# Output projection of a hybrid encoder layer on one Trainium2 core: a PSUM bank of its own for the second half of each normalized tile's transposition, both halves one product later, and three gating steps later

## Chip, core and metric

The kernel runs on one core of one Trainium2 chip. The metric is device time in microseconds (us). The engines are named as in the profile: PE is the matrix engine (PEld its weight loads), DVE the vector engine, ACT the scalar engine, POOL the GpSimd engine, SP the engine that issues most DMAs. PSUM, where PE writes its results, has eight banks of 128 x 512 numbers here.

## What is computed

The reference is one encoder layer over 1280 tokens (256 and 1024) of width 1024:

```python
h = rmsnorm(x, attn_norm_g)
proj = h @ w_in
a = mla_group(...)            # latent attention, 8 heads
b = na_group(...)             # neighbourhood attention, 8 heads
mix = concatenate([rmsnorm(a, mla_out_g), rmsnorm(b, na_out_g)])
x = x + mix @ w_o             # output projection
h2 = rmsnorm(x, ffn_norm_g)
x = x + (silu(h2 @ w_gate) * (h2 @ w_up)) @ w_down
y = rmsnorm(x, final_norm_g)
```

The change lies between `mix @ w_o` and the first products with `w_gate` and `w_up`.

## The kernel before

Every matmul operand is kept as a high and a low part, and one product is three matmuls (`mm3`, lines 111 to 113). Tokens go in ten tiles of 128. The instructions of ACT, DVE and POOL are put in order by a scheduler when the kernel is built; PE's order is as written from the second turn of the output projection to the end of the first feed-forward run. Each engine executes its own queue strictly in order; engines wait for one another by semaphores. The names below are those of the profile.

**Output projection.** Turn t (t from 0 to 9) of a loop multiplies tile t's mixed, transposed activations `mT` with `wo`: 16 products `at` = 0 to 15, each of three matmuls into bank `po` (two buffers; the first eight products fill one half of the columns, the last eight the other). A dictionary `between` says what PE does after which product. In turn t that is, for the next tile's mixed activations, the transposition of a first half after product 1 and of a second half after product 5 (four 128 x 128 transposes each, line 898, into the single bank `trm`), which ACT (line 900) and DVE (line 901) read out; and for the tile before, t - 1, the transposition of its normalized activations `h2`, again in two halves, after products 9 and 12 (line 957, into the single bank `trh`). DVE multiplies the first half into the feed-forward input `x` (line 961), ACT the second half (line 967).

What the normalized tile needs is a chain over four engines: PE ends the tile's products, DVE adds the residual (line 930), ACT squares and sums (line 941), POOL makes the factor `rh` (lines 90 and 92), DVE scales the tile (line 944), and only then PE can transpose. POOL's queue holds much other work in this stage, above all weight operands for the feed-forward (lines 1064, 1069, 1071). DVE's queue holds sums over tiles (lines 984 and 992) as well. For the last two tiles the second half goes into `trm`; the last tile's two halves come when the feed-forward run has begun, in `xm_in`.

**Feed-forward.** Gate and up products come in runs of 20 pairs (steps `at`), a run for each of the two matrices and each block of columns; they use a seven-fold scheme with sums of operands (`S`, made by `build_S`), and PSUM banks `M` (pools `pm0` and `pm1`, four buffers each; `pm1` takes the banks that `po`, `trm` and `trh` had). DVE adds what a bank holds into the result tile `C` (line 1239), ACT copies where the result is first written (line 1241). `C` has three buffers. While the run after the first two goes on (n = 0 in `plan`), DVE works through the gating of the finished pair: `act_step` (lines 1266 and 1272) with the numbers in `STEPS_1`, each ordered after the eviction next to it, and SP stores the results (`act_d`). One bank of `M`, called `junk`, is held during the output projection as a dump for ACT's squares (line 881).

Of the kernel before, what the change touches and what calls it, by code (L numbers as in the profile page):

```python
# [12 lines left out]
F32 = mybir.dt.float32  # L13
# [6 lines left out]
P = 128  # L20
# [3 lines left out]
NT = NTOK // P  # L24
# [16 lines left out]
def encoder_trunk(ctx: ExitStack, tc: tile.TileContext, x_tm, x_T, g_attn, w_c, w_v, w_qk,  # L41
# [14 lines left out]
    def pool(name, bufs=1, side=None, space=None):  # L56
        kw = {"reuse_waits": "tile"}
        if side:
            kw["side"] = side
        if space:  # L60
            kw["space"] = space
        return tc.alloc_tile_pool(name=name, bufs=bufs, **kw)

    def load(out, in_):
        nc.sync.dma_start(out=out, in_=in_)

    def store(out, in_):
        nc.scalar.dma_start(out=out, in_=in_)
# [7 lines left out]
    def load_r(out, in_):  # L76
        nc.sync.dma_start(out=out.bitcast(F32), in_=in_.bitcast(F32))
# [10 lines left out]
    def rstd_of(out, ss, n):  # L88
        w = out.shape[1]
        nc.gpsimd.tensor_scalar(out=out, in0=ss, scalar1=1.0 / n, scalar2=EPS,  # L90
                                op0=ALU.mult, op1=ALU.add)
        return nc.gpsimd.tensor_tensor(out=out, in0=out, in1=mhalf[:, 0:w], op=ALU.pow).ins
# [70 lines left out]
    def load_x(t):  # L163
        x = rx.tile([P, D], F32, name="x", bufs=2)
        load(x, x_tm[t * P:(t + 1) * P, :])
        return x
# [684 lines left out]
    po = pool("po", space=PSUM, side="right")  # L851
# [6 lines left out]
    def load_wo(n, pl, nm):  # L858
        raws = pl.tile([P, 2, D], F32, name=nm)
        for j in range(2):  # L860
            kc, raw = 2 * n + j, raws[:, j]
            load(raw, w_o[kc])
            nc.gpsimd.tensor_scalar(out=raw, in0=raw, scalar1=gm[:, kc:kc + 1], scalar2=1.0,
                                    op0=ALU.mult, op1=ALU.mult)
            wt = rw.tile([P, 2, D], F32R, name=f"wo{kc}")
            split_w(wt[:, 0], wt[:, 1], raw)
            wo.append(wt)
# [23 lines left out]
    def mix_T(t, mn):  # L891
        mT = (rt1 if t % 2 else rt0).tile([P, 2, KC, P], F32R, name=f"mT{t % 2}")

        def half(q):
            tr = po.tile([P, 4, P], F32, name="trm", bufs=1)
            for i in range(4):
                kc = 4 * q + i
                nc.tensor.transpose(tr[:, i], mn[:, kc * P:(kc + 1) * P], ident)
            hi, lo = mT[:, 0, 4 * q:4 * q + 4], mT[:, 1, 4 * q:4 * q + 4]
            last_split[0] = nc.scalar.copy(out=hi, in_=tr).ins  # L900
            last_low[0] = nc.vector.tensor_sub(out=lo, in0=tr, in1=hi).ins

        return mT, half
# [33 lines left out]
    def ffn_in(t, x):  # L937
        h2 = rm.tile([P, D], F32, name="m", bufs=3)
        ss = rm.tile([P, 1], F32, name="ssh", bufs=2)
        r = rm.tile([P, 1], F32, name="rh", bufs=2)  # L940
        nc.scalar.activation(h2, x, AF.Square, accum_out=ss)
        store(xm_d[t], x)
        normed[0] = rstd_of(r, ss, D)
        scaled[0] = nc.vector.tensor_scalar(out=h2, in0=x, scalar1=r, scalar2=1.0, op0=ALU.mult,
                                            op1=ALU.mult).ins
        cuts, a = [], t * P
        while a < (t + 1) * P:
            j = a // XC
            e = min((j + 1) * XC, (t + 1) * P)
            cuts.append((j, slice(a - j * XC, e - j * XC), slice(a - t * P, e - t * P)))  # L950
            a = e

        def half(q):
            tr = po.tile([P, 4, P], F32, name="trm" if t >= NT - 2 and q else "trh", bufs=1)
            for i in range(4):
                kc = 4 * q + i
                tp = nc.tensor.transpose(tr[:, i], h2[:, kc * P:(kc + 1) * P], ident)
            for j, to, of in cuts:
                if q == 0:
                    for k in range(2):  # L960
                        ev[0] = nc.vector.tensor_mul(
                            out=X[k, j][:, :, to], in0=tr[:, 2 * k:2 * k + 2, of],
                            in1=gf[:, 2 * k:2 * k + 2].unsqueeze(2).to_broadcast(
                                [P, 2, of.stop - of.start])).ins
                else:
                    for i in range(4):
                        nc.scalar.activation(X[2 + i // 2, j][:, i % 2, to], tr[:, i, of],
                                             AF.Copy, scale=gf[:, 4 + i:5 + i])
            return tp.ins

        return half
# [61 lines left out]
    pm = [pool("pm0", space=PSUM)]  # L1033
    for n, (pl, nm) in enumerate(((rw, "wo4"), (rw, "wo5"), (rw, "wo6"), (rt0, "mT0"))):
        load_wo(n, pl, nm)
    junk = [None, pm[0].tile([P, 512], F32, name="M0", bufs=4)]
    cur, half = mix_T(0, mix_in(0))
    half(0)
    half(1)
# [46 lines left out]
    last_half = None  # L1086
    for t in range(NT):
        if t == 1:
            pe_order.enter_context(tc.manual_schedule(engines={mybir.EngineType.SP,
                                                               mybir.EngineType.PE}))  # L1090
        if t + 2 < NT:
            with tc.issue_after(last_split[0]):
                coming = mix_in(t + 2)
        x = load_x(0) if t == 0 else x_next
        x_next = load_x(t + 1) if t + 1 < NT else None
        for job in kept:
            load_r(*job)
        kept.clear()
        if t < 3:
            k = (slice(4, 6), slice(0, 4), slice(6, 8))[t]  # L1100
            for i in range(2):
                load(raw[:, i, k], src[i][0][:, k])
        with tc.issue_after(mixed[0]):
            for _ in range(2 if 1 < t < 6 else 1):
                next(early, None)
        jobs = JOBS.get(t, (None,) * 3)
        halves_[0] = t < NT - 1
        if t == NT - 1:
            with tc.issue_after(scaled[0]):
                for job in SECOND[4:5] + SECOND[6:]:  # L1110
                    job()
        between = {}
        if t + 1 < NT:
            nxt, half_m = mix_T(t + 1, ahead)

            def second_m(half_m=half_m, jobs=jobs):
                half_m(1)
                behind_now(last_low[0], jobs[0])

            between[1] = lambda: half_m(0)  # L1120
            between[5] = second_m
        if t:
            def first_h(half=last_half, jobs=jobs):
                half(0)
                behind_now(ev[0], jobs[2])
                if t == 8:
                    behind_now(ev[0], jobs[3])

            between[9 if t < 9 else 8] = first_h
            between[12 if t < 9 else 11] = lambda half=last_half: half(1)  # L1130
        if t < NT - 1:
            between[7] = lambda jobs=jobs: behind_now(added[0], jobs[1])
        out_proj(t, cur, x, between)
        if t == NT - 1:
            break
        last_half = ffn_in(t, x)
        with tc.issue_after(normed[0]):
            next(early, None)
            if t == 8:
                third_2(gps, slice(0, 168))  # L1140
        cur, ahead = nxt, coming
# [12 lines left out]
    last_half = ffn_in(9, x)  # L1154

    def xm_in(q):
        last_half(q)
        if q == 0:
            return
        for p_ in reversed(r3):  # L1160
            p_.release()
        po.release()
        pm.append(pool("pm1", space=PSUM, side="right"))
        l4.append(pool("l4t"))
# [163 lines left out]
    for at in range(20):  # L1328
        if at and at + 3 < 20:
            load_r(ring[(at + 3) % 4], wop_d[SEQ0[at + 3][0]])  # L1330
        if at in (5, 7):
            load_raw(1, at == 7)
        if at in BUILD:
            with tc.issue_after(evicted[0]):
                build_S(BUILD[at])
        w = ring[at % 4]
        for i, C in enumerate((G, U)):
            product(C, chains[i], written[i], SEQ0, at, (w[:, 0, i], w[:, 1, i]), BANK.get(at))
            if (at, i) in ((2, 1), (3, 0)):
                xm_in(at - 2)  # L1340
    pe_order.close()
    gate(G, 1)
    gate(G, 0)
# [91 lines left out]
    def advance(now):  # L1435
        while done[0] < len(jobs):
# [8 lines left out]
            if k == 8 and m + 2 < len(plan):  # L1445
# [3 lines left out]
    STEPS = {(0, 0): ((0, 1), 3), (0, 1): (1,), (0, 2): (7,), (0, 4): (2,), (0, 8): (5,),  # L1449
             (0, 12): (6,), (1, 12): ("22", 4), (1, 16): ("12",), (1, 18): ((0, 0),),  # L1450
             (1, 19): ((0, 2),)}
    STEPS_1 = {1: ("22", 4), 2: ("12",), 4: (7,), 8: ("11", 3), 10: (1,), 12: ("21",), 16: (2,)}
    STEPS_2 = {1: (5,), 4: (6,)}
    for n, (fp, i) in enumerate(plan):
        C = new_C()
# [12 lines left out]
        for at in range(20):  # L1468
# [7 lines left out]
            product(C, chains, written, seq, at, w)  # L1476
            steps_ = () if last_one else STEPS_1.get(at, ()) if n == 0 else STEPS.get((i, at), ())
            with tc.issue_after(evicted[0]):
# [302 lines left out]
```

## Time and profile before

| | us |
|---|---|
| three timed runs | 1599.02, 1597.18, 1597.21; median 1597.21 |
| profiled execution, its own time | 1599.25 |
| its span, first to last instruction | 1597.2 |

| engine | busy us of the span | share |
|---|---|---|
| PE | 1559.9 | 98% |
| DVE | 1015.4 | 64% |
| ACT | 761.1 | 48% |
| POOL | 766.1 | 48% |

The output projection lies at about 660 to 803 us of the span, the first feed-forward run at 803 to 850, the run n = 0 at 850 to 875. Timeline rows of the profile give start and duration in us, engine, line, operation, output from inputs, shapes and count, and in brackets the idle time ahead of the row with what ended it.

### The profile page before, as it was taken

The page shows a single profiled execution, that of the slowest core. Times are in us where ns is not written, and L with a number is a line of the kernel's source. Part 1 is how long each engine was busy: PE and PEld are TensorE (multiplying, and loading weights), DVE is VectorE, ACT ScalarE, POOL GpSimd, SP SyncE. Part 2 cuts the span into 40 slices and gives each one's busy share as a digit, 9 for nine tenths or more (in the row PEclk, how much of TensorE's full clock was granted, in tenths as well). Part 3 has the DMA queues.
Part 4 walks back from the last instruction along what each step waited for, and adds up shares of the span by engine and source line. Part 5 has one row for each costly group of instructions (what it writes and reads, how often), then busy time and mean ns, then how long its engine had stood idle before and what let it go on. Part 6 is the DMA issues. An engine that isn't in the chain of part 4 may idle for free.

```text
span 1597.2 us, 23983 instructions
## 1 busy us (share of the span) xinstructions
PE 1559.9 (98%) x8560; PEld 1395.4 (87%) x8560; DVE 1015.4 (64%) x1656; ACT 761.1 (48%) x1552; POOL 766.1 (48%) x961
## 2 busy tenths in 40 slices
PE   8999999999999999998999999999999999999998
PEld 8888789998888888877798999999999988888886
DVE  5754034566777777535588666566766665886676
ACT  6533144555677777633344444444344453443334
POOL 4633235544211119369536887788888871010002
PEclk9999999999999999999999999999999999999999
DMA  8626022253101030276473222223322237843434
GB/s 292 200 73 167 17 55 62 38 175 100 32 16 31 21 101 29 87 256 216 157 256 112 93 94 86 80 107 111 103 85 94 86 131 278 293 125 100 150 104 156
DMA packets 118022, 190.38 MB, mean 119 GB/s; under 512 B 34960, under 2 KB 65424, under 8 KB 115344
## 3 DMA queue, kind: packets, MB, share of 16 engines
q1 hardware_dynamic: 85216, 162.64, 31.2%
q10 hardware_dynamic: 31872, 23.14, 4.6%
q0 software_dynamic: 816, 3.08, 0.5%
q8 instruction: 67, 1.10, 0.3%
q14 instruction: 51, 0.42, 0.1%
HBM read 128.92 MB, written 59.90 MB: 118 GB/s over the span
## 4 chain that ended last, share of the span: by engine, by line
PE 84%; DVE 4%; POOL 4%; DMA 3%; ACT 2%; issue 2%; SPq 0%; ACTq 0%; POOLq 0%; DVEq 0%
PE M L112 10%; PE M L113 10%; PE M L111 10%; PE d L111 6%; PE d L113 6%; PE d L112 6%; PE o L789 4%; PE tp L779 4%; PE na_o L513 3%; PE pj L111 2%; PE pj L112 2%; PE pj L113 2%; PE S L111 2%; PE S L113 2%; PE S L112 2%
## 5 line engine op out<-in xcount | busy, mean ns | idle before, releaser
L1239 DVE TENSOR_TENSOR C<-M,C 128x428 f32<-128x428 f32 (+1 forms) x263 | 150.9, 594 | 145.5 <-PE M L113 74.8
L1020 POOL TENSOR_TENSOR wr<-wt,wr 128x512 fp32r<-128x512 f32 (+1 forms) x106 | 149.3, 1409 | 68.3 <-ACT wr L1018 68.1
L1018 ACT CAST wr<-wt 128x512 fp32r<-128x512 f32 (+1 forms) x106 | 63.2, 599 | 132.9 <-PE M L112 123.7
L111 PE MATMUL M<-s,wr 128*128 128x428 f32 x352 | 125.7, 357 | 0.1
L112 PE MATMUL M<-s,wr 128*128 128x428 f32 x352 | 125.4, 356 | 0.1
L113 PE MATMUL M<-s,wr 128*128 128x428 f32 x352 | 125.2, 357 | 0.0
L101 DVE TENSOR_TENSOR PT<-tp,PT 128x512 fp32r<-128x512 f32 (+1 forms) x144 | 93.4, 658 | 35.4 <-ACT PT L100 34.1
L1241 ACT COPY C<-M 128x428 f32<-128x428 f32 (+1 forms) x128 | 63.3, 513 | 85.3 <-PE M L113 85.3
L111 PE MATMUL M<-x,wr 128*128 128x428 f32 x264 | 94.3, 357 | 2.0 <-DVE C L1239 1.8
L100 ACT CAST PT<-tp 128x512 fp32r<-128x512 f32 (+1 forms) x144 | 79.4, 568 | 33.4 <-PE tp L779 30.1
L802 POOL TENSOR_TENSOR ob<-ob 128x128 f32<-128x128 f32 x40 | 18.5, 463 | 158.6 <-ACT ob L799 143.7
L771 DVE TENSOR_REDUCE mm<-S 128x1 f32<-128x1024 f32 (+1 forms) x80 | 84.9, 1062 | 13.7 <-PE S L113 12.2
L113 PE MATMUL M<-x,wr 128*128 128x428 f32 x264 | 91.4, 357 | 0.5 <-POOL wr L1020 0.3
L112 PE MATMUL d<-SE 128*128 128x512 f32 (+1 forms) x238 | 91.8, 387 | 0.0
L111 PE MATMUL d<-SE 128*128 128x512 f32 (+1 forms) x238 | 89.6, 388 | 0.0
L113 PE MATMUL d<-SE 128*128 128x512 f32 (+1 forms) x238 | 89.6, 387 | 0.0
L1281 ACT CAST SE<-as 128x640 fp32r<-128x640 f32 x58 | 42.2, 727 | 95.4 <-issue 57.2
L773 ACT ACTIVATE ex<-S,mm 128x1024 f32<-128x1024 f32 (+1 forms) x80 | 79.8, 998 | 14.8 <-DVE mm L771 13.5
L779 PE MATMUL tp<-ident,ex 128*128 128x128 f32 x544 | 79.2, 274 | 2.4 <-DVE PT L101 1.3
L789 PE MATMUL o<-PT,v 128*128 128x256 f32 x544 | 80.6, 287 | 0.8 <-ACT PT L100 0.8
L90 POOL TENSOR_SCALAR ry<-ssy 128x1 f32<-128x1 f32 x5 | 4.1, 817 | 157.6 <-ACT yo L1571 157.5
L111 PE MATMUL M<-SE,wr 128*128 128x428 f32 x220 | 78.6, 357 | 0.7 <-DVE C L1239 0.7
(464 smaller groups left out, 4908.3 us busy)
## 6 DMA issues: line engine op xcount, KB each, us to landing
as<-act_d SPq DMA_DIRECT2D x73, 320.0 KB
act_d<-C SPq DMA_DIRECT2D x70, 320.0 KB
w<-in_w_down_dram SPq DMA_DIRECT2D x44, 256.0 KB
x<-in_x_tm_dram SPq DMA_DIRECT2D x20, 512.0 KB
wr<-wop_d SPq DMA_DIRECT2D x20, 512.0 KB
wraw<-in_w_gate_dram SPq DMA_DIRECT2D x10, 1024.0 KB
wraw<-in_w_up_dram SPq DMA_DIRECT2D x10, 1024.0 KB
wop_d<-wr SPq DMA_DIRECT2D x18, 512.0 KB
```

The source lines that it names most:

```text
L100: i = nc.scalar.copy(out=hi, in_=ps)
L101: nc.vector.tensor_sub(out=lo, in0=ps, in1=hi)
L111: nc.tensor.matmul(out, lhsT=sh, rhs=mh, start=first, stop=False, **kw)
L112: nc.tensor.matmul(out, lhsT=sh, rhs=ml, start=False, stop=False, **kw)
L113: return nc.tensor.matmul(out, lhsT=sl, rhs=mh, start=False, stop=last, **kw).ins
L771: nc.vector.reduce_max(out=nm[:, u:u + 1], in_=S, axis=AX.X, negate=True)
L773: nc.scalar.activation(ex, S, AF.Exp, bias=nm[:, u:u + 1], scale=1.0, accum_out=l[:, u:u + 1])
L779: nc.tensor.transpose(tp[:, j], ex[:, kt * P:(kt + 1) * P], ident)
L789: nc.tensor.matmul(oT, lhsT=vv, rhs=pt[s][g][:, j], start=kt == 0 and s == 0, stop=kt == nkt - 1 and s == 1)
L1020: i1 = (eng or nc.gpsimd).tensor_tensor(out=lo, in0=raw_, in1=hi, op=SUB)
L1239: evicted[0] = nc.vector.tensor_add(out=o, in0=ps[:, 0:XN[j]], in1=o).ins
L1241: nc.scalar.copy(out=o, in_=ps[:, 0:XN[j]])
```

## The change

The second half of tiles 0 to 7 is transposed into another buffer of `M`, also held during the output projection. In turns 1 to 8 the two halves come after products 10 and 13. The last tile's halves come one product later. In `STEPS_1` three entries move from steps 10, 12 and 16 to 11, 14 and 17.

```diff
         def half(q):
-            tr = po.tile([P, 4, P], F32, name="trm" if t >= NT - 2 and q else "trh", bufs=1)
+            if q and t < NT - 2:
+                tr = junk[2].rearrange("p (a b) -> p a b", a=4)
+            else:
+                tr = po.tile([P, 4, P], F32, name="trm" if q else "trh", bufs=1)
...
-    junk = [None, pm[0].tile([P, 512], F32, name="M0", bufs=4)]
+    junk = [None] + [pm[0].tile([P, 512], F32, name="M0", bufs=4) for _ in range(2)]
...
-            between[9 if t < 9 else 8] = first_h
-            between[12 if t < 9 else 11] = lambda half=last_half: half(1)
+            between[10 if t < 9 else 8] = first_h
+            between[13 if t < 9 else 11] = lambda half=last_half: half(1)
...
-            if (at, i) in ((2, 1), (3, 0)):
-                xm_in(at - 2)
+            if at == 3:
+                xm_in(i)
...
-    STEPS_1 = {1: ("22", 4), 2: ("12",), 4: (7,), 8: ("11", 3), 10: (1,), 12: ("21",), 16: (2,)}
+    STEPS_1 = {1: ("22", 4), 2: ("12",), 4: (7,), 8: ("11", 3), 11: (1,), 14: ("21",), 17: (2,)}
```

On POOL and SP the order of instructions is the same. On PE, in turn 5, from the first half of tile 4 to its second, before (`po` is the product, `trh` the transposition):

```order
L957 MATMUL trh<-ident,m 128x128 [waits DVE_49,Activation_49]
L957 MATMUL trh<-ident,m 128x128 x3
L111 MATMUL po<-wo_8158,mT_8709 128x512
L112 MATMUL po<-wo_8158,mT_8709 128x512
L113 MATMUL po<-wo_8158,mT_8709 128x512
L111 MATMUL po<-wo_8163,mT_8709 128x512
L112 MATMUL po<-wo_8163,mT_8709 128x512
L113 MATMUL po<-wo_8163,mT_8709 128x512
L111 MATMUL po<-wo_8169,mT_8709 128x512
L112 MATMUL po<-wo_8169,mT_8709 128x512
L113 MATMUL po<-wo_8169,mT_8709 128x512
L957 MATMUL trh<-ident,m 128x128 [waits DVE_49,PE_49]
```

And now (lines behind the edit are three higher):

```order
L960 MATMUL trh<-ident,m 128x128 [waits DVE_49]
L960 MATMUL trh<-ident,m 128x128 x3
L111 MATMUL po<-wo_8163,mT_8707 128x512
L112 MATMUL po<-wo_8163,mT_8707 128x512
L113 MATMUL po<-wo_8163,mT_8707 128x512
L111 MATMUL po<-wo_8169,mT_8707 128x512
L112 MATMUL po<-wo_8169,mT_8707 128x512
L113 MATMUL po<-wo_8169,mT_8707 128x512
L111 MATMUL po<-wo_8174,mT_8707 128x512
L112 MATMUL po<-wo_8174,mT_8707 128x512
L113 MATMUL po<-wo_8174,mT_8707 128x512
L960 MATMUL M_8189<-ident,m 128x128 [waits Activation_49]
```

Both halves stand one product later, and the second half no longer waits for DVE, which reads the first half, but for ACT, which read the bank a tile ago.

On PE in the first feed-forward run, the last tile's two halves (`trh`, then `trm`) before, where the products with `s_9378` are those of step 3, for gate and for up:

```order
L957 MATMUL trh<-ident,m 128x128 [waits DVE_49,PE_49]
L957 MATMUL trh<-ident,m 128x128 x3
L111 MATMUL M_9397<-s_9378,wr_9371 128x428 [waits DMAHW6_49,Activation_49]
L112 MATMUL M_9397<-s_9378,wr_9371 128x428
L113 MATMUL M_9397<-s_9378,wr_9371 128x428
L111 MATMUL M_9397<-s_9378,wr_9371 128x428
L112 MATMUL M_9397<-s_9378,wr_9371 128x428
L113 MATMUL M_9397<-s_9378,wr_9371 128x428
L957 MATMUL trm<-ident,m 128x128 x4
L111 MATMUL M_9406<-s_9378,wr_9371 128x428
L112 MATMUL M_9406<-s_9378,wr_9371 128x428
L113 MATMUL M_9406<-s_9378,wr_9371 128x428
```

And now:

```order
L960 MATMUL trh<-ident,m 128x128 [waits DVE_49,PE_49]
L960 MATMUL trh<-ident,m 128x128 x3
L111 MATMUL M_9399<-s_9371,wr_9364 128x428
L112 MATMUL M_9399<-s_9371,wr_9364 128x428
L113 MATMUL M_9399<-s_9371,wr_9364 128x428
L111 MATMUL M_9399<-s_9371,wr_9364 128x428
L112 MATMUL M_9399<-s_9371,wr_9364 128x428
L113 MATMUL M_9399<-s_9371,wr_9364 128x428
L960 MATMUL trm<-ident,m 128x128 x4
L111 MATMUL M_9488<-s_9374,wr_8113 128x428 [waits DMAHW0_49,Activation_49]
L112 MATMUL M_9488<-s_9374,wr_8113 128x428
```

The up product of step 3 now stands between the two halves, so that the product of step 4, which opens a new bank and waits for ACT, comes straight behind the second half.

On DVE in the run n = 0 (L1239 is an eviction from the bank named, L1266 and L1272 the gating, L1020 a weight's low part), before:

```order
L1239 TENSOR_TENSOR C_9802<-M0_9838,C_9802 128x428 [waits PE_49]
L1272 TENSOR_TENSOR C_9387<-C_9388 128x640 [waits DVE_49]
L1239 TENSOR_TENSOR C_9802<-M0_9814,C_9802 128x428 [waits DVE_49,PE_49]
L1266 TENSOR_TENSOR C_9388<-C_9388,C_9387 128x640
L1020 TENSOR_TENSOR wr0_8113<-wraw_8112,wr0_8113 128x512 [waits DMAHW6_49,Activation_49]
L1239 TENSOR_TENSOR C_9802<-M0_9927,C_9802 128x428 [waits DVE_49,PE_49]
L1272 TENSOR_TENSOR C_9387<-C_9388 128x640 [waits DVE_49]
L1239 TENSOR_TENSOR C_9802<-M0_9838,C_9802 128x428 [waits PE_49,Activation_49]
L1239 TENSOR_TENSOR C_9802<-M0_9814,C_9802 128x428 [waits DVE_49,PE_49]
```

And now:

```order
L1242 TENSOR_TENSOR C_9795<-M0_9831,C_9795 128x428 [waits PE_49]
L1242 TENSOR_TENSOR C_9795<-M0_9807,C_9795 128x428 [waits DVE_49,PE_49]
L1275 TENSOR_TENSOR C_9380<-C_9381 128x640
L1023 TENSOR_TENSOR wr0_8113<-wraw_8112,wr0_8113 128x512 [waits DMAHW6_49,Activation_49]
L1242 TENSOR_TENSOR C_9795<-M0_9920,C_9795 128x428 [waits DVE_49,PE_49]
L1242 TENSOR_TENSOR C_9795<-M0_9831,C_9795 128x428 [waits PE_49,Activation_49]
L1242 TENSOR_TENSOR C_9795<-M0_9807,C_9795 128x428 [waits DVE_49,PE_49]
L1269 TENSOR_TENSOR C_9381<-C_9381,C_9380 128x640
L1023 TENSOR_TENSOR wr3_9364<-wraw_8112,wr3_9364 128x512 [waits DMAHW1_49,Activation_49]
```

Of the second and the fourth eviction of before, the second now stands ahead of the gating step that was in front of it, and the fourth has one gating step less in front.

## The prediction

> **What bounds the kernel now.** I read the page first, then the windows by stage, then who waited for whom on PE, and then the rows of the engines behind each wait.
>
> ```profile
> span 1597.2 us, 23983 instructions
> ...
> 690.00:830.00 140.00, 131.25 (x640) 108.95 (x640) 80.62 (x122) 54.43 (x124) 91.97 (x108) 0.99 0.60 216
> 713.89:766.07 52.18, 45.06 (x213) 35.84 (x213) 27.54 (x42) 18.78 (x48) 49.34 (x53) 0.97 0.60 216
> ...
> 755.50:758.20 2.70, 2.70 (x14) 2.00 (x13) 2.70 (x4) 0.47 (x2) 2.62 (x3) 1.00 0.66 193
> 758.20:762.00 3.80, 1.29 (x6) 1.22 (x6) 3.49 (x7) 1.05 (x2) 3.53 (x5) 0.84 0.69 277
> 762.00:764.00 2.00, 2.00 (x6) 1.57 (x5) 0.27 (x1) 1.00 (x4) 1.99 (x2) 0.50 0.47 146
> ...
> 880.00:1580.00 700.00, 698.64 (x3387) 634.38 (x3386) 478.80 (x647) 284.75 (x485) 378.40 (x314) 1.00 0.37 126
> ```
>
> The columns are length, then busy time of PE, PEld, DVE, ACT, POOL, then PE's granted clock. From 880 to 1580 PE is busy for 698.64 of 700 us, so what PE gains ahead of 880 stays to the end. In the stage that the change touches it idles 8.75 of 140 us. POOL, off the critical path by the shares of the page, is full from 714 to 766 (49.34 of 52.18, the rest being gaps between its instructions).
>
> ```profile
> PE trh L957 <- DVE x L961: 6.1, 3, 2.6
> PE trh L957 <- DVE m L944: 2.5, 4, 0.8
> PE M L111 <- DVE C L1239: 2.1, 2, 1.4
> ```
>
> These are PE's waits between 690 and 880: us in total, times, longest. The first is the second half waiting until DVE has read the first half out of the same bank; the second is the first half waiting for the normalized tile; the third lies in the run n = 0. The change touches all three. Their 10.7 us are therefore the ceiling, together with a slow clock that I come to; the question is what of it comes back as another wait.
>
> ```profile
> 739.94 0.63 PE L957 MATMUL trh<-ident,m 128*128 128x128 f32 x4 [0.80 <-DVE m L944]
> ...
> 745.24 0.63 PE L957 MATMUL trh<-ident,m 128*128 128x128 f32 x4 [2.58 <-DVE x L961]
> ...
> 749.18 0.60 PE L898 MATMUL trm<-ident,m 128*128 128x128 f32 x4
> ...
> 755.56 0.60 PE L957 MATMUL trh<-ident,m 128*128 128x128 f32 x4
> ...
> 760.76 1.06 PE L957 MATMUL trh<-ident,m 128*128 128x128 f32 x4 [2.51 <-DVE x L961]
> ...
> 766.29 0.60 PE L898 MATMUL trm<-ident,m 128*128 128x128 f32 x4
> ...
> 769.51 0.60 PE L898 MATMUL trm<-ident,m 128*128 128x128 f32 x4
> ```
>
> These are turns 5 and 6. From 745.24 to 749.18 PE does four transposes and five products, 3.94 us; a product is 0.71 and a transposition 0.38. The same work from 760.76 takes 5.53 us.
>
> ```profile
> 752.94 0.56 POOL L92 TENSOR_TENSOR rh<-rh,mhalf 128x1 f32<-128x1 f32 x1
> ...
> 767.11 0.19 POOL L90 TENSOR_SCALAR rh<-ssh 128x1 f32<-128x1 f32 x1 [1.04 <-ACT m L941]
> ```
>
> ```profile
> 753.53 1.77 DVE L944 TENSOR_SCALAR m<-x,rh 128x1024 f32<-128x1024 f32 x1 [2.40 <-POOL rh L92]
> ...
> 759.88 0.74 DVE L961 TENSOR_TENSOR x<-trh,gf 128x256 f32<-128x256 f32 x2
> 760.92 1.35 DVE L984 TENSOR_TENSOR SE<-x,SE 128x428 fp32r<-128x428 f32 x2 [0.31 <-ACT SE L982]
> 765.09 0.69 DVE L930 TENSOR_TENSOR x<-po,x 128x512 f32<-128x512 f32 x1 [2.82 <-PE po L113]
> 767.54 0.69 DVE L901 TENSOR_TENSOR mT<-trm,mT 128x512 fp32r<-128x512 f32 x1 [1.76 <-ACT mT L900]
> ```
>
> ```profile
> 765.87 1.06 ACT L941 ACTIVATE m<-x 128x1024 f32<-128x1024 f32 x1 [2.87 <-issue]
> ...
> 766.92 0.59 ACT L900 CAST mT<-trm 128x512 fp32r<-128x512 f32 x1
> ```
>
> **The change, part by part.** *Turns 1 to 5.* POOL's queue fixes when tile 5 is normalized, whatever PE does: L92 at 752.94 has no idle ahead of it, DVE's L944 follows at 753.53 and ends at 755.30, and PE can transpose at about 755.45 (0.15 behind, as 739.94 lies behind other work). So what PE gains in turns 2 to 5 (2.58 in turn 5 and the remaining 6.1 - 2.58 - 2.51 = 1.0 ahead of it for second halves, 2.5 - 0.66 = 1.8 for first halves, 0.66 being the last tile's below) only brings it earlier to that point, where it waits. The first half then starts at 755.45 against 755.56, with eleven products done and not ten: 0.71 + 0.11 = 0.82 us gained, no more.
>
> *Turn 6.* The second half has its own bank and finds it free: its reader is ACT, a tile ago. The 2.51 us of idle time go, start to start 760.76 less (755.56 + 0.38 + 3 products of 0.71) = 2.69. The slow stretch behind it goes too, if the clock stays up: 5.53 - 3.94 = 1.59.
>
> *What is late next.* DVE works without a pause from 753.53 to 760.62 (2.70 of 2.70 and 3.49 of 3.80 us in the windows) and then has L984 until 762.27, none of which PE's gain moves. The add L930, which stood behind PE at 765.09, now finds PE done at about 759.8 but DVE busy: it starts at 762.27 and ends at 762.9. ACT's L941 follows, then L900 1.05 later (765.87 to 766.92), at 764.05, then L901 0.62 behind L900, at 764.65 to 765.35. The bank `trm` is free only then. PE is there at 755.45 + 0.38 + 3 x 0.71 + 0.36 + 4 x 0.71 + 3.22 (from 766.29 to 769.51) = 764.4. So the second mixing transposition of turn 7 waits a new 0.95 us. POOL, at 767.11 idle for 1.04 before, is ready about as early as DVE then needs it, 766.1; the first half of turn 7 comes at about 769.2 and finds its tile. I find nothing later in turns 7 to 9 that doesn't move with PE.
>
> Net of the output projection: 0.82 + 2.69 - 0.95 = 2.56 us, and 1.59 more against an execution that had the slow stretch. The bounds are 0.8, if the second-half gain comes back whole, and 3.5, if there is no new wait.
>
> ```profile
> 810.78 0.63 PE L957 MATMUL trh<-ident,m 128*128 128x128 f32 x4 [0.66 <-DVE m L944]
> ...
> 812.43 0.60 PE L957 MATMUL trm<-ident,m 128*128 128x128 f32 x4
> ...
> 814.26 0.46 PE L111 MATMUL M<-s,wr 128*128 128x428 f32 x1
> ```
>
> ```profile
> 813.07 1.14 ACT L967 ACTIVATE x<-trm,gf 128x128 f32<-128x128 f32 x4 [4.74 <-PE trm L957]
> ```
>
> ```profile
> 826.46 0.19 PEld L112 LDWEIGHTS M<-s,wr 128*128 128x128 f32 x1 [0.43 <-DVE s L984]
> ```
>
> *The last tile's halves.* The 0.66 in front of the first half goes, hidden by a product (1.27 between the two halves, 812.43 less 810.78 and 0.38, and about 0.1 less where none is in front). But the second half now stands right ahead of the product that opens a bank of `pm1`, which ACT must have read out: from 812.43 to 814.26 are 1.83 us, which a product covered before. The old order takes 0.66 + 3.48 = 4.14 us to 814.26, the new one 1.17 + 0.38 + 1.27 + 1.83 = 4.65: a loss of 0.5. The scheduler puts the operand that PE waited for at 826.46 ahead of two evictions, so that this 0.43 goes. Together I count nothing, within -1.5 (ACT comes later as well) and +0.9 (both waits go without a new one).
>
> ```profile
> 867.03 1.40 DVE L1272 TENSOR_TENSOR C<-C 128x640 f32<-128x640 f32 x1
> 868.36 0.59 DVE L1239 TENSOR_TENSOR C<-M,C 128x428 f32<-128x428 f32 x1
> 868.87 1.38 DVE L1266 TENSOR_TENSOR C<-C 128x640 f32<-128x640 f32 x1
> 870.18 1.77 DVE L1020 TENSOR_TENSOR wr<-wraw,wr 128x512 fp32r<-128x512 f32 x1
> ...
> 872.39 0.84 DVE L1272 TENSOR_TENSOR C<-C 128x640 f32<-128x640 f32 x1
> 873.15 1.30 DVE L1239 TENSOR_TENSOR C<-M,C 128x428 f32<-128x428 f32 x2
> ```
>
> ```profile
> 869.00 0.46 PE L111 MATMUL M<-SE,wr 128*128 128x428 f32 x1 [0.73 <-DVE C L1239]
> ...
> 873.80 0.47 PE L111 MATMUL M<-x,wr 128*128 128x428 f32 x1 [1.42 <-DVE C L1239]
> ```
>
> *The gating steps.* PE waited at 869.00 for the eviction of 868.36, which stood behind a gating step of 1.40 us. That step is now behind it: the eviction can start at 867.1 and the wait goes (0.73 idle). The eviction of 873.15 then has L1272, L1020 and an eviction in front instead of L1266, L1020, an eviction and L1272: it ends near 867.7 + 1.4 + 1.77 + 1.1 = 872.0, where PE, 0.73 earlier, asks for it at 871.65. 0.35 of 1.42 stays. Gain 0.73 + 1.07 = 1.8, between 0.6 (if DVE is as late for the second) and 2.7 (both, start to start).
>
> **The sum.** No instruction and no DMA is added, and their number and durations stay. Without the slow stretch 2.56 + 0 + 1.8 = 4.35 us. The profiled execution took 1599.25 (its span and 2.05 around it) and had the stretch: 1599.25 - 4.35 - 1.59 = 1593.3. The timed runs are 1599.02, 1597.18 and 1597.21; two clusters 1.8 apart, near the 1.59 that the stretch costs, make me estimate that the median is an execution without it: 1597.21 - 4.35 = 1592.9, which I take. 0.2% is 3.2 us, about what a measurement of this kernel tells from no change.
>
> **The clock.** The windows row shows PE at half clock from 762 to 764, right behind 2.51 us of idle time, while 2.58 us of idle time at 745.24 left the next rows at full speed. The Trainium skill (TensorE: Matmul & The Clock Gate, "What's actually happening") says that the clock halves after an idle window of about 3.4 us, that the window runs freely and that its phase differs from run to run. The trace agrees on the half clock and on a run's chance, but not on the idle time needed, since 2.51 us were enough. By that rule alone the changed kernel, with a longest idle time well under 3.4 us, would not slow down, and the sum would be 1592.9.
>
> **The rivals.**
> - *The gain is taken back in turns 7 and 8.* POOL's and DVE's queues are full until 766, and the second half's 2.69 us come back as waits of the mixing halves or of L944. For it: POOL's 49.34 of 52.18. Against it: POOL idled 1.04 at 767.11. Then 0.82 + 1.8 = 2.6 us: 1594.6. Chance 0.22.
> - *The clock drops again.* In turns 4, 6 and 7 PE still idles 1 to 2 us each, and a window may catch enough of it: 1592.9 + 1.6 = 1594.5. Against it: no idle time as long as 2.51 remains. Chance 0.12.
> - *More is gained.* No new wait in turn 7, both waits of the run n = 0 go: 3.5 + 2.7 + 0.2 = 6.4 us, 1590.8. Chance 0.14.
> - *Slower.* The next run's results go into the buffer of `C` from which steps 7, 1 and 2 are stored, so ACT's first copy into it waits for those stores; step 2 now ends DVE's list.
>
> ```profile
> 873.26 14.46 SPq L65 DMA_DIRECT2D act_d<-C  x3
> ...
> 880.93 0.52 ACT L1241 COPY C<-M 128x428 f32<-128x428 f32 x1
> ...
> 751.07 3.34 DMA m<-a_d
> ```
>
> The store, issued at 873.26 before, would be issued at about 876.8 and, with the 3.34 us of the nearest transfer on the chain, land at 880.1; the copy would be ready at 879.1. A wait of 1.0 us on ACT is still ahead of PE's next use of that bank. To end above 1600.4 it would have to cost 7.5 us, a landing time of some 11. Chance 0.04.
>
> **How the numbers follow.** My forecast has 0.48 (1592 to 1594). Faster by over 0.2%, below 1594.0: nearly all of that, the third rival, and a few hundredths of the first two, 0.62. Within 0.2%: 0.34. Slower: 0.04. The range runs from the third rival's 1590.8 to 1595.2, past the first two at 1594.6 and 1594.5 by the 0.6 by which the last tile's halves may cost more.
>
> **What would show it.** Right: no wait of `trh` or `M` for DVE's L961; one wait of 1 to 2.5 us for L944 in turn 6 and under 1 us in turn 5; a wait of about 1 us at the second mixing half of turn 7; about 1.5 us between the last tile's second half and the next product; one wait of some 0.3 us in the run n = 0. Wrong: waits for L944 in turns 7 to 9, several waits for evictions between 820 and 900, a stretch at half clock, or PE idle behind 880 on a copy that waits for `act_d`.

## The result, and the profile after

The changed kernel takes 1594.36 us (median of 14 runs, 1592.50 to 1595.70), the kernel before, run beside it, 1597.85 (14 runs, 1597.00 to 1599.33): 3.5 us less between the medians; the ratio is 0.9976 with a 95% interval from 0.9968 to 0.9985. The time is inside the predicted range and 1.5 us above the predicted 1592.9. The profiled execution took 1593.86.

The page gives the span:

```profile
span 1591.8 us, 23991 instructions
```

The windows of the stage and of its fullest part (length, busy time of PE, PEld, DVE, ACT and POOL, PE's clock, DMA):

```profile
690.00:830.00 140.00, 134.41 (x665) 112.28 (x664) 86.10 (x129) 54.82 (x125) 91.59 (x108) 1.00 0.64 225
713.00:765.00 52.00, 48.16 (x235) 37.82 (x234) 27.93 (x42) 20.41 (x52) 49.21 (x53) 1.00 0.63 227
```

PE idles 5.6 of the 140 us, where it idled 8.75. The clock stays up (1.00 in both rows). POOL is as full as it was (49.21 of 52). PE's waits between 690 and 880 (us in total, times, longest):

```profile
PE trh L960 <- DVE m L944: 2.2, 3, 1.0
PE M L111 <- ACT x L970: 1.2, 1, 1.2
PE trm L898 <- DVE mT L901: 1.0, 2, 0.6
PE M L111 <- DVE C L1242: 1.0, 1, 1.0
PE trm L898 <- POOL m L886: 0.9, 1, 0.9
PE M L111 <- ACT C L1244: 0.3, 1, 0.3
```

The largest of the old waits, 6.1 us for DVE's readout, is gone. New ones stand in its place: for the readout by ACT (the last tile), for the mixing halves' bank (L901), for POOL's normalized mixing tile (L886), and a small one for ACT in the run n = 0. Lines from 954 on are three higher than before: L957 is L960, L961 is L964, L1239 is L1242 and so on.

PE's rows of turns 5 to 7, from the timeline; the wait ahead of a row stands in its brackets:

```profile
739.10 0.66 PE L960 MATMUL trh<-ident,m 128*128 128x128 f32 x4 [0.95 <-DVE m L944]
741.69 0.60 PE L960 MATMUL M<-ident,m 128*128 128x128 f32 x4
745.93 0.66 PE L898 MATMUL trm<-ident,m 128*128 128x128 f32 x4 [0.87 <-POOL m L886]
749.77 0.63 PE L898 MATMUL trm<-ident,m 128*128 128x128 f32 x4 [0.41 <-DVE mT L901]
754.65 0.66 PE L960 MATMUL trh<-ident,m 128*128 128x128 f32 x4 [0.83 <-DVE m L944]
757.23 0.60 PE L960 MATMUL M<-ident,m 128*128 128x128 f32 x4
760.67 0.65 PE L898 MATMUL trm<-ident,m 128*128 128x128 f32 x4
764.75 0.63 PE L898 MATMUL trm<-ident,m 128*128 128x128 f32 x4 [0.64 <-DVE mT L901]
```

The second half, now in a bank `M`, starts 2.6 us behind the first in both turns, as it should with three products between. What holds the first half of turn 6 back is seen in the timelines of POOL and of DVE:

```profile
752.23 0.56 POOL L92 TENSOR_TENSOR rh<-rh,mhalf 128x1 f32<-128x1 f32 x1
```

```profile
752.83 1.76 DVE L944 TENSOR_SCALAR m<-x,rh 128x1024 f32<-128x1024 f32 x1 [3.21 <-POOL rh L92]
```

DVE idles 3.21 us until POOL has made the factor `rh`. POOL has no idle time ahead of that row; its L92 comes at 752.23, where it came at 752.94 before.

A measure used below: the time from the second mixing half of turn 2 to that of turn 7, 694.65 to 769.51 before, 74.86 us, and 694.55 to 764.75 after, 70.20. (The expectations call its start turn 1; by the rows it is turn 2's, and the waits for L944 that they place in turn 1 are in turn 2.)

The timelines of the run n = 0, first PE, then DVE, POOL and ACT:

```profile
867.70 0.46 PE L111 MATMUL M<-x,wr 128*128 128x428 f32 x1 [0.98 <-DVE C L1242]
...
879.98 0.46 PE L111 MATMUL M<-SE,wr 128*128 128x428 f32 x1 [0.34 <-ACT C L1244]
```

```profile
861.76 1.29 DVE L1242 TENSOR_TENSOR C<-M,C 128x428 f32<-128x428 f32 x2
862.97 1.95 DVE L1275 TENSOR_TENSOR C<-C 128x640 f32<-128x640 f32 x1
864.85 1.77 DVE L1023 TENSOR_TENSOR wr<-wraw,wr 128x512 fp32r<-128x512 f32 x1
866.55 1.81 DVE L1242 TENSOR_TENSOR C<-M,C 128x428 f32<-128x428 f32 x3
```

```profile
862.96 1.28 POOL L1023 TENSOR_TENSOR wr<-wt,wr 128x512 fp32r<-128x512 f32 x1
```

```profile
875.41 0.52 ACT L1244 COPY C<-M 128x428 f32<-128x428 f32 x1 [0.54 <-PE M L113]
...
878.47 0.62 ACT L1021 CAST wr<-wt 128x512 fp32r<-128x512 f32 x1 [1.39 <-POOL wt L1029]
879.00 0.93 ACT L1244 COPY C<-M 128x428 f32<-128x428 f32 x2
```

One of the two old waits is gone, the other is still 0.98, and there is a new one of 0.34: ACT's two evictions at 879.00 stand behind a cast that waited 1.39 us for a sum of POOL. Below, a product is named by its operand: the one of 867.70 is the product 'x', that of 879.98 the product 'SE'. Aligned product by product, PE is 4.78 us ahead of the kernel before at the start of this run, 6.10 at 'x' and 5.62 at 'SE'.

### The profile page after: what moved, and what is told of

Its sections match the earlier page's. It is cut to its first block, busy times and chain, and to the rows that moved or that the text cites. A ratio compares the mean times of both kernels' runs of the same rounds, so it can differ in the third digit from the quotient of the medians.

```text
span 1591.8 us, 23991 instructions
## 1 busy us (share of the span) xinstructions
PE 1559.4 (98%) x8560; PEld 1394.9 (88%) x8560; DVE 1016.4 (64%) x1656; ACT 760.2 (48%) x1552; POOL 766.4 (48%) x961
## 4 chain that ended last, share of the span: by engine, by line
PE 83%; POOL 6%; DMA 3%; DVE 3%; ACT 3%; issue 2%; SPq 0%; POOLq 0%; ACTq 0%; DVEq 0%
PE M L113 10%; PE M L111 10%; PE M L112 10%; PE d L111 6%; PE d L113 6%; PE d L112 6%; PE o L789 4%; PE tp L779 3%; PE na_o L513 3%; PE pj L111 2%; PE pj L112 2%; PE pj L113 2%; PE S L111 2%; PE S L113 2%; PE S L112 2%
## 5 line engine op out<-in xcount | busy, mean ns | idle before, releaser
L1242 DVE TENSOR_TENSOR C<-M,C 128x428 f32<-128x428 f32 (+1 forms) x263 | 151.0, 594 | 144.0 <-issue 68.1
```

What stands on the lines that cost most here:

```text
L1242: evicted[0] = nc.vector.tensor_add(out=o, in0=ps[:, 0:XN[j]], in1=o).ins
```

## The experiments

Each ratio is to runs of the kernel before on the same chip and in the same hour. Runs of one kernel spread over 1 to 6 us, so where little is in question the rows of the profile decide.

**1. The own bank alone.**

```diff
-            tr = po.tile([P, 4, P], F32, name="trm" if t >= NT - 2 and q else "trh", bufs=1)
+            if q and t < NT - 2:
+                tr = junk[2].rearrange("p (a b) -> p a b", a=4)
...
-    junk = [None, pm[0].tile([P, 512], F32, name="M0", bufs=4)]
+    junk = [None] + [pm[0].tile([P, 512], F32, name="M0", bufs=4) for _ in range(2)]
```

> Own bank for the second half alone; halves behind products 9 and 12, the last tile and the gating steps as before. Theory (only the readout wait matters): the three waits for DVE's readout in turns 3, 5 and 6 (0.97 + 2.58 + 2.51) go, and what POOL's queue fixes (L944 in turns 1, 5, 6) does not move whether the first half stands behind product 9 or 10, so the whole gain of the output projection is there: 3.0 us less than the kernel before, with waits for L944 in turns 1, 3, 5 and 6 that are up to 0.65 longer than in the changed kernel, and the wait of about 0.6 for the mixing half of turn 7 gone or smaller. Rival (the later place is half of it): one product, 0.65, more is lost in turn 6 and in the turns before it, and the gain is 2.3 or less.

Measured: 1595.09 us against 1597.23, ratio 0.9986 (0.9977 to 0.9995), 2.2 us less. PE's rows of turn 6 and the window between them:

```profile
756.38 0.66 PE L960 MATMUL trh<-ident,m 128*128 128x128 f32 x4 [2.07 <-DVE m L944]
760.53 0.60 PE L960 MATMUL M<-ident,m 128*128 128x128 f32 x4
```

```profile
758.00:760.00 2.00, 2.00 (x6) 1.54 (x5) 2.00 (x3) 0.00 (x0) 1.91 (x2) 0.50 0.99 369
```

No readout wait is left, but the wait for L944 in turn 6 is 2.07, not 0.83, and behind it the clock is at 0.50: from the first to the second half are 4.15 us instead of 2.6. From turn 2 to turn 7 it takes 71.83, 1.63 more than in the changed kernel's profile, and the slow stretch is 1.57 of that. The interval, 0.8 to 3.7 us less, holds the theory's 3.0 and the rival's 2.3 alike. My theory took the first half's later place for worthless, since POOL fixes the end. PE waits as much in turn 6 as in the changed kernel, 2.2 us to 2.1 in all; but there it waits in three pieces (0.87, 0.41, 0.83), and here nearly all at once. That the later places are worth something because short waits leave the clock up is what this one execution suggests, not more.

**2. The later places alone.**

```diff
-            between[9 if t < 9 else 8] = first_h
-            between[12 if t < 9 else 11] = lambda half=last_half: half(1)
+            between[10 if t < 9 else 8] = first_h
+            between[13 if t < 9 else 11] = lambda half=last_half: half(1)
```

> Halves behind products 10 and 13 alone, both still in trh's bank; the rest as before. Theory (DVE reads the first half out at a time that its own queue fixes): the readout waits stay and the second halves of turns 5 and 6 start when they did, with one product less behind each: 0.65 us gained per such turn, about 1.3 us less than the kernel before, between 0.6 and 2. Rival A (POOL's queue sets the turns): no gain, 0.0 to 0.3. Rival B (the wait is mostly for L944, so one product later removes it and the readout wait with it): 2.5 us or more.

Measured: 1595.86 us, ratio 0.9992 (0.9983 to 1.0001), 1.3 us less, the size of the theory, but no change is inside the interval. The profile has readout waits of 0.37, 2.57 and 1.14, with half clock behind the 2.57, and 71.88 us from turn 2 to turn 7. What the later places do by themselves stays open.

**3. The gating steps alone.**

```diff
-    STEPS_1 = {..., 8: ("11", 3), 10: (1,), 12: ("21",), 16: (2,)}
+    STEPS_1 = {..., 8: ("11", 3), 11: (1,), 14: ("21",), 17: (2,)}
```

> The three gating steps later, alone. By the prediction's working 1.8 us less than before. By the comparison of the two traces 0.8: the wait at the product 'SE' goes, that at the product 'x' shrinks by 0.4 only, and a new one of 0.3 comes some 12 us later, where ACT's evictions stand behind a cast that waits for a sum of POOL. Rival (the new waits come from the last tile's new place and not from the steps): 1.8. The output projection has its waits for L961 as before; whether the stretch of half clock of turn 6 comes again says if it belongs to the idle time or to chance.

Measured: 1595.43 us, ratio 0.9994 (0.9985 to 1.0003). The interval holds no change, so the rows must decide. Aligned with the kernel before, PE is 3.27 us ahead at the start of the run n = 0, 4.60 at the product 'x' and 4.14 at the product 'SE': 0.87 us, not 1.8. The new wait (0.31 here) is there without any change to the last tile, so the steps bring it. The output projection is that of the kernel before, and yet ran otherwise, as PE's rows of turns 5 and 6 and a window of turn 5 show:

```profile
743.74 0.63 PE L957 MATMUL trh<-ident,m 128*128 128x128 f32 x4 [2.57 <-DVE x L961]
749.24 0.60 PE L898 MATMUL trm<-ident,m 128*128 128x128 f32 x4
...
759.26 0.63 PE L957 MATMUL trh<-ident,m 128*128 128x128 f32 x4 [1.00 <-DVE x L961]
```

```profile
745.00:747.00 2.00, 2.00 (x7) 1.51 (x6) 0.00 (x0) 1.35 (x4) 2.00 (x3) 0.50 0.03 8
```

Here the half clock came in turn 5 (5.50 us from 743.74 to 749.24 instead of 3.94). PE is later by that, so the wait of turn 6 is 1.00 instead of 2.51, and turn 2 to turn 7 takes 71.96, not 74.86. In turn 5 the slow stretch costs nothing, since a wait follows that absorbs it.

**4. The last tile put back.**

```diff
-            if at == 3:
-                xm_in(i)
+            if (at, i) in ((2, 1), (3, 0)):
+                xm_in(at - 2)
```

> The changed kernel with the last tile's halves behind the product pairs 2 and 3 as before. Theory (the two effects cancel): the first product into M1 comes 0.3 to 0.5 us earlier than in the changed kernel, the wait of 0.4 for an operand 12 us later comes back, and the time is that of the changed kernel within 0.2. Rival (the new wait of 1.2 us for ACT's readout is a net loss): 0.4 to 1.2 us less than the changed kernel, at every place after the first product into M1.

Measured: 1593.63 us, ratio 0.9977 (0.9967 to 0.9986), as the changed kernel. Against the changed kernel PE goes from 2.07 to 2.39 us ahead at the first product into `M1` (a bank of `pm1`) and back to 2.04 behind the operand's wait, which returns (the row is one of PE's weight loads):

```profile
819.70 0.19 PEld L112 LDWEIGHTS M<-s,wr 128*128 128x128 f32 x1 [0.43 <-DVE s L987]
```

The two effects of the last tile cancel, as predicted.

**5. POOL's early operands spread.** Turns 4 and 5 issue one of them each, not two; the two left over move to turns 6 and 7.

```diff
-            for _ in range(2 if 1 < t < 6 else 1):
+            for _ in range(2 if 1 < t < 4 else 1):
                 next(early, None)
```

> The changed kernel, in which turns 4 and 5 issue one early operand of POOL each instead of two (as turns 0, 1, 6 and 7 do; the two that are left over come in turns 6 and 7). Theory (POOL's queue sets turns 5 and 6): L92 and L944 of turns 4 and 5 end 2 us or more earlier against the turn, PE's waits for L944 in front of the first halves of turns 5 and 6 (0.95 and 0.83 in the changed kernel) go, those in front of the mixing halves of turns 6 and 7 (0.87, 0.41, 0.64) go or shrink below 0.5 in all, and the time from the second mixing half of turn 1 to that of turn 7 falls from 70.2 (or 68.5, as the run with the tail undone had it) to 66 to 67: 2 to 4 us less than the changed kernel. Rival A (DVE's queue of sums is as full): waits for DVE stay, 1 us or less is gained. Rival B (the two operands that move make turns 7 and 8 late): 2 us gained by turn 7 and 1 to 2 lost again before the last tile.

Measured: 1589.91 us against 1597.97, ratio 0.9948 (0.9936 to 0.9961). That is 4.5 us less than the changed kernel by the two ratios. All of PE's waits between 690 and 815, then the factor and L944 of tile 5, for turn 6, in the timelines:

```profile
PE M L111 <- ACT x L970: 1.2, 1, 1.2
PE trh L960 <- DVE m L944: 0.2, 1, 0.2
```

```profile
746.16 0.56 POOL L92 TENSOR_TENSOR rh<-rh,mhalf 128x1 f32<-128x1 f32 x1
```

```profile
746.76 1.78 DVE L944 TENSOR_SCALAR m<-x,rh 128x1024 f32<-128x1024 f32 x1 [0.58 <-POOL rh L92]
```

The waits of the mixing halves, named for DVE and POOL, went with those for L944. Turn 2 to turn 7 takes 65.05 us, and nothing is lost in turns 8 and 9 (108.38 us from turn 2 to the last tile's second half, 113.49 in the changed kernel). POOL's queue set turns 5 to 7.

**6. The last tile's halves exchanged:** `last_half(1 - q)` for `last_half(q)`, so that ACT's half goes first.

> The changed kernel with the last tile's two halves exchanged: the half that ACT reads out first, the one that DVE reads out right ahead of the first product into M1. Theory (that product waits for ACT's readout of 1.14 us and its start-up): from the later half to that product 1.2 us instead of 1.84, so 0.5 us less than the changed kernel there, as long as DVE's queue lets the readout through at once. Rival (DVE has evictions in front of the readout): the wait is as long or longer, 0 to 1 us lost. Over the whole program both are within what the runs can tell; the rows of the profile decide.

Measured: 1593.67 us, ratio 0.9976 (0.9966 to 0.9987), no difference that the runs could tell. In the rows the first product into `M1` comes 0.36 us behind the later half, with no wait at all: it waits only for `trm`, whose readout is then over, and not for the half that DVE reads. Of 1.5 us gained there 0.9 are left 11 us later.

**7. The gating steps later still.**

```diff
-    STEPS_1 = {..., 8: ("11", 3), 11: (1,), 14: ("21",), 17: (2,)}
+    STEPS_1 = {..., 8: ("11", 3), 14: (1,), 17: ("21",), 18: (2,)}
```

> The changed kernel with the gating steps of the run n = 0 later still (1 behind product 14, '21' behind 17, 2 behind 18), so that none stands on DVE in front of the three evictions that PE waits for at the product 'x' (0.98 of idle time). Theory (POOL's queue of weight operands is next): that wait goes or falls below 0.3, and the one at the product 'SE' 12 us later, 0.34 idle, grows to 1.2 to 1.5, since ACT's evictions there stand behind a cast that waits for POOL: net gain over the changed kernel 0.2 or less. Rival (the step was what cost it): 1.0 to 1.2 us gained for good.

Measured: 1596.67 us, ratio 0.9990 (0.9981 to 0.9998), by the ratios some 2 us more than the changed kernel, though the intervals overlap; neither theory had this. ACT's row and PE's from the timelines:

```profile
874.68 0.93 ACT L1244 COPY C<-M 128x428 f32<-128x428 f32 x2 [3.84 <-DMA act_d<-C]
```

```profile
875.25 0.46 PE L111 MATMUL M<-s,wr 128*128 128x428 f32 x1 [1.98 <-ACT C L1244]
```

The wait at the product 'x' went, with 1.0 us gained. But ACT's first eviction into the reused buffer of `C` now waited 3.84 us for the stores of the steps, PE 1.98 for that bank, and the clock fell behind it: 3.2 us lost, 2.2 net. This is the mechanism of the prediction's slower rival, brought on by steps later than the change put them. Whether POOL's operands come next could not be seen here.

**8. The same, and two evictions of the run n = 1 by DVE** (`nc.vector.tensor_copy` for `nc.scalar.copy` in its second product).

> The same, and in the run n = 1 the two evictions of the second product are made by DVE, which idles there, in place of ACT, where they stand behind the cast that waits for POOL. Theory: both waits go (0.98 and 0.34 idle, 1.15 and 0.5 from start to start), 1.4 to 1.7 us less than the changed kernel at the product 'SE' and after it. Rival (POOL's operands themselves are late): PE then waits for a weight operand instead, and the net gain is 0.5 or less.

Measured: 1595.83 us, ratio 0.9985 (0.9976 to 0.9994). The same wait for the stores, 2.63 us of PE, hides the rest. A miss as a test; experiment 10 repeats it with the steps in their places.

**9. Experiments 5 and 6 together.**

> The changed kernel with both edits that gained: one early operand of POOL in turns 4 and 5, and the last tile's halves exchanged. They lie 20 us apart and share no queue that was full, so the theory is that they add: 4.5 + 1.0 = 5.5 us less than the changed kernel, 9.0 less than the kernel before. Rival (with the turns earlier, DVE's evictions stand in front of the exchanged half): the exchange gains less than 0.3, 8.1 less than before in all.

Measured: 1588.66 us against 1597.45, ratio 0.9944 (0.9932 to 0.9957), 8.8 us less than before. The exchange itself gained 1.5 us and lost most of it again, by this row of PE,

```profile
813.79 0.46 PE L111 MATMUL M<-SE,wr 128*128 128x428 f32 x1 [0.62 <-DVE C L1242]
```

to an eviction that stands behind DVE's sums, themselves later by the half exchanged: 0.35 us is left, and nothing in the next kernel (1.07 of wait there). The rival's mechanism holds for the exchange.

**10. The same with the two evictions of experiment 8.**

> The same, and the two evictions of the second product of the run n = 1 made by DVE instead of ACT; the gating steps stand as in the changed kernel. Theory (the wait of 0.34 in front of the product 'SE' comes from ACT's evictions standing behind the cast that waits for POOL): it goes, 0.4 to 0.5 us less from there on, and the idle time of 0.98 before it stays. Rival A (POOL's operands are the limit): PE waits for a weight operand there instead, gain under 0.2. Rival B (DVE's copies of about 0.58 us stand behind its gating steps): a wait for DVE of 0.3 or more takes its place.

Measured: 1588.45 us, ratio 0.9945 (0.9932 to 0.9957). The wait at the product 'SE' is gone and PE is 0.50 us further ahead of the changed kernel there (4.65 to 5.15), as the theory had it: ACT's order was its cause, and POOL's operands were not late themselves. The whole time cannot show so little. Experiments 9 and 10 have the lowest medians; their intervals overlap with each other and with experiment 5's, so the runs do not tell the three apart.

**11. The kernel before, with POOL's operands spread and nothing else.**

> The kernel before with POOL's early operands spread as in f1 and nothing else. Theory (two separate causes in the output projection: POOL's lateness, and the shared bank): L944's waits in turns 5 and 6 go, but the readout waits in turns 5 and 6 stay with 1 to 1.9 us each, since DVE reads the first half out near 740.7 and 753.5 where the second half would want to start near 739 and 752: the time from the second mixing half of turn 1 to that of turn 7 comes to 68 to 69.5 (f1 with its own bank: 65.1), 2.5 to 4 us less than before. Rival (POOL's lateness was all of it): 66 or less, and the bank of its own would have been worth nothing with POOL's queue spread.

Measured: 1592.71 us, ratio 0.9969 (0.9957 to 0.9982): 4.7 us less than the kernel before. The change itself brings 3.5, and the two intervals overlap. Its waits between 690 and 815:

```profile
PE trh L957 <- DVE x L961: 1.6, 2, 0.8
PE trh L957 <- DVE m L944: 0.9, 2, 0.6
```

Turn 2 to turn 7 takes 65.90, where the rival had 66 or less, and where the profiles of the changed output projection have 68.15 to 70.28. The readout waits shrink from 6.1 to 1.6 with the banks as they were. They too came mostly from POOL: a late L944 sets DVE's whole queue back, the readout in it (in the kernel before DVE has no pause from the end of L944 at 755.30 to the readout at 759.88). With POOL's queue spread, the own bank and the later places together are worth 0.85 us up to turn 7 (65.90 against 65.05), and a wait of 0.80 in turn 8.

**12. The kernel before once more.**

> The kernel before, one more profile. Theory (PE's clock halves behind one of the two long waits of 2.5 us, and if it does so in turn 5, turn 6 waits that much less): either the stretch of half clock is in turn 5, the wait for the readout in turn 6 is about 1.0, and turn 1 to turn 7 takes 72, or it is in turn 6, behind a wait of 2.5, and it takes 74 to 75. Rival (the stretch comes by chance, apart from the waits): none or another place, 72.5 to 73.5 with 2.5 of waiting in both turns.

Measured: 1599.76 us, and 74.90 from turn 2 to turn 7. PE's second halves of turns 5 and 6, and a window behind each:

```profile
745.72 0.63 PE L957 MATMUL trh<-ident,m 128*128 128x128 f32 x4 [2.59 <-DVE x L961]
...
761.28 0.92 PE L957 MATMUL trh<-ident,m 128*128 128x128 f32 x4 [2.55 <-DVE x L961]
```

```profile
747.00:749.00 2.00, 2.00 (x11) 1.60 (x10) 0.52 (x1) 1.32 (x4) 2.00 (x3) 1.00 0.03 8
...
762.00:764.00 2.00, 2.00 (x6) 1.61 (x6) 0.79 (x2) 1.14 (x4) 2.00 (x2) 0.50 0.31 78
```

The second case of the theory: full clock behind the wait of turn 5, half behind that of turn 6. With experiment 3 and the first profile, three executions of this output projection each had one slow stretch, in turn 6 twice (74.9) and in turn 5 once (72.0).

## Why the prediction was right, and where not

- *Turns 1 to 5* were to come to 0.82 us at turn 6's first half: 0.11 by an earlier start and 0.71 by the one product more that is done ahead of it. The start moved by 0.91, from 755.56 to 754.65. The stage began 0.11 earlier, so 0.80 remain, and with the product 1.51. The path is right: PE waits there for L944, and experiment 5 shows that POOL's queue is the cause. What failed is that this queue fixes the time "whatever PE does": L92, put at 752.94, came at 752.23. From turn 2's second mixing half to this half are 60.10 us here and 58.04 to 60.17 in the five profiles with this output projection (58.44 in experiment 4), where the three of the kernel before's have 60.90 to 61.14. Why POOL differs from execution to execution stays open. The wait for L944 was to be 1 to 2.5 us; it is 0.83, since PE had already waited 0.87 and 0.41 in the same turn.
- *Turn 6's second half*, predicted 2.69: from 760.76 to 757.23, less the 0.91, 2.62. Right against this execution. Experiment 3 had a wait of only 1.00 there to take away.
- *The new wait of turn 7*, predicted 0.95, from DVE's queue: 0.64 of idle time, and 0.86 by the rows (5.62 ahead at 760.67, 4.76 at 764.75). Right. Those of 0.87 and 0.41 in turn 6 I did not have; they come from the same queue of POOL.
- *The slow stretch*, priced at 1.59, cost 1.38: from turn 6's second half to the next mixing half the kernel before does five products and the changed one four, so 5.53 less 0.71 stands against 3.44. The three profiles of the kernel before's output projection do not show an execution without it, as I assumed for the median; one has it where it costs nothing.
- *The net of the output projection*, 2.56 without the stretch's price, came out, but by luck. Against experiment 3 (71.96) the five profiles with the changed output projection (68.15 to 70.28, mean 69.30) gain 2.7 us. There turns 1 to 5 gave 2.7 on the mean and turn 6's second half only 1.1, and some 1.1 was given back in turn 7; the prediction had 0.82, 2.69 and 0.95.
- *The last tile's halves*, predicted as nothing: 0.33 us lost at the first product into `M1`, 0.4 regained behind it. Right.
- *The gating steps* are the other term that was far off: 1.8 predicted, 0.84 by the rows (0.87 in experiment 3). The first wait went. For the second I had 0.35 left, by "867.7 + 1.4 + 1.77 + 1.1 = 872.0", with the step at its old 1.40 us; it took 1.95, and 0.98 stayed. And I had not looked at the engine that follows: ACT's evictions behind the cast that waits for POOL, 0.5 us of PE from start to start.
- *The rivals.* The measured time lies beside the first rival's 1594.6, but not by its mechanism: nothing was taken back in turns 7 and 8 beyond the predicted wait. The clock did not drop in the changed kernel's profile. The slower rival did not come (at 875.41 above ACT waits for PE alone), though the room was small: with the steps put still later, in experiment 7, it cost 3.2 us.

With the measured sizes the sum is 2.7 + 0 + 0.9 = 3.6 us, against the 3.5 between the medians. The forecast of 4.35 came near it because turns 1 to 5 gave more than was priced, where turn 6 and the gating steps gave less. What the prediction named but did not use is that POOL's queue was the cause: I priced its end as given, and by moving two of its operands the runs gained 4.5 us more.

## What to carry to other kernels

Where a wait is removed and another engine's queue fixes the next meeting point, the gain ends there; the edit that pays is in that queue, even if that engine is hardly on the chain. Follow a wait back until an engine without idle time comes: here PE waited for DVE's readout, DVE for POOL, and spreading two operands of POOL shrank both waits, while the separate bank treated the last link only. And before a step is put later, look for the buffer that it keeps busy, since its store may be what the next run waits for.

## What was not expected of the hardware

**The clock fell behind waits of 2 us.** Nine waits of PE between 1.98 and 2.63 us stand in the profiles of this stage and of the run n = 0. Behind seven of them the granted clock went to 0.50 (2.51 and 2.55 in turn 6; 2.57 twice in turn 5; 2.07, 1.98 and 2.63 in experiments 1, 7 and 8). Behind the other two, 2.58 and 2.59, it did not, and the next long wait, 15 us later, brought it. Behind waits of 1.42 or less it never fell there. Each time the half clock lasted 3.4 us, by the windows' means (in experiment 12, 0.67 over 0.80 us, 0.50 over 2.00 and 0.78 over the next 2.00 give 0.5 + 2.0 + 0.9). The Trainium skill (TensorE: Matmul & The Clock Gate, "What's actually happening") gives 3.4 us as the length of the free-running window; the length agrees, while its wholly idle window is more than was needed here.

**A step of DVE was held up by POOL, and the wait stands in its duration.** DVE's row of 862.97 starts 0.01 us behind POOL's of 862.96, which ends at 864.24; it ends at 864.92, 0.68 later. Before, the step of 867.03 ended at 868.43, which is 0.68 behind the end (867.75) of the first of these two rows of POOL, while the second took 1.85 instead of 1.28 (the kernel before, timeline of POOL):

```profile
865.88 1.87 POOL L1026 TENSOR_TENSOR wt<-wraw 128x512 f32<-128x512 f32 x1
867.72 1.85 POOL L1020 TENSOR_TENSOR wr<-wt,wr 128x512 fp32r<-128x512 f32 x1
```

The Trainium skill (SBUF — State Buffer, "Who interferes with whom") says that a DVE instruction with two SBUF inputs contends with a POOL instruction that reads SBUF, and calls this contention an exclusive lock; these rows agree. So the 1.40 us that I carried over as the step's price was 0.7 of work and 0.7 of POOL's instruction, and belonged to its place.
